# A hybrid decoder layer on one core: when the second attention's keys and queries are scaled

## The chip, the cores and the metric

The kernel runs on one core of one Trainium2 chip. The metric is the device time of one execution in microseconds (us); the number for a kernel is the median of its runs. A profile is one execution with every instruction's start and duration. Engines are named as in the profile: PE is the matrix engine and PEld its weight load, DVE the vector engine, ACT the scalar engine, POOL the GpSimd engine, SP the engine that issues most of the DMAs.

## What is computed

One layer on x of 512 tokens by 1024 features, in float32. The input is normed and multiplied by one wide matrix, whose columns feed four branches: a forgetting attention (8 heads of 64), a gated linear recurrence, a sparse attention (8 query heads on 2 key heads, over compressed blocks, selected blocks and a window), and a spatial gating unit. Each branch is gated, projected and added up, and one output projection is added to x. The change touches the sparse attention only:

```python
def rms_norm(x, g):
    x32 = x.astype(jnp.float32)
    y = x32 * lax.rsqrt(jnp.mean(x32 * x32, axis=-1, keepdims=True) + NORM_EPS)
    return (y * g.astype(jnp.float32)).astype(x.dtype)
...
y_c = nsa_attention(rms_norm(heads(qc, NSA_HEADS), qn_c), ..., kn_c, ...)
    # inside: rms_norm(k_slc, kn_g) and rms_norm(k_win, kn_g)
```

So 8 query heads and 4 key heads (2 selected, 2 window) of each token are divided by their root mean square.

## The kernel before

**Products.** Every float32 matrix product is made of three passes over pairs of rounded parts (high by high, low by high, high by low). A unit of dense work is three matmuls of 128x128 weights on 512 columns; the code counts it as `G` = 0.68. A dense product of the input matrix (`zgen` or `chunks`) loads a weight half by DMA into a raw buffer, rounds it to the high part on POOL or ACT (`hi_cast`), makes the low part by a subtraction on DVE (`wsplit`), and runs its units; the last unit of a bank is followed by its eviction.

**Two attentions with dense work between.** The first attention (`fox_units`, tiles `s_a`, `p_a`, `o_a`) and the second (`nsa_units`, tiles `s_s`, `p_s`, `s_w`, `p_w`, `o_s`) are chains of small steps on all engines. A call `fill(us)` puts so many microseconds of dense units from a queue between two steps (`step` takes one). Small jobs (generators in the list `side`) advance by one `yield` with each dense unit. In the queue during the first attention stand, in order, the keys and values `kv` (bank `z_kv`), the queries `qc` (bank `z_qc`), `cm0` (`z_cm`), `vd` (`z_vd`), then `ga`, and behind the first attention more `ga`, `gd` and `ud`.

**The order.** Within both attentions the instructions are not issued as they are written. `Order.add` collects them with what each needs; `Order.plan` walks a model of the engines in time and on each engine takes, among the instructions that can start, the one written first; `Order.settle` issues the result. The engines run their queues in this order, so an instruction that comes later than the model thought holds up everything behind it on its engine. The first settle is at the end of the first attention (`shut(r1)`), the second at the end of the second.

**What the change touches.** `emit_kv` and `emit_z` copy keys (`zkm`, rows named `zk_c` in the code) and queries (`zq_c`) out of their banks on ACT, square them on ACT (`sq`) and sum each head's squares on DVE into `ssc`. `nsa_scales` then makes 48 inverse roots per token row: a scaling of `ssc` and eleven small dependent DVE instructions of `rsqrt` on the tile `tsc`, and then eight POOL multiplications that scale keys and queries in place, four of 256 and four of 512 elements per partition. In the kernel before it is called behind the first attention:

```python
    kts = [k_tiles(rp2, nm) for nm in "sw"]
    nsa_scales()
    ...
    side.append(compress())
    later(*silu("ga", y["a"], range(2, 4)), *(zgen(f"gd{i // 2}", i % 2, gd_use(i)) for i in range(4)),
          *(zgen(f"ud{i // 2}", i % 2, ud_use(i)) for i in range(4)))
    fill(5 * G)
    k_operand(zk_c, 0, KNC, kts[0], "s")
    fill(2 * G)
    q0 = q_operand(zq_c, 0, QNC, "c0")
    fill(6 * G)
```

`k_operand` and `q_operand` turn the scaled keys and queries on PE (`kt_s`, `qt_c`) and make the attention's operands of them on ACT, DVE and POOL (`ka_s`, `kb_s`, `q_c`). `compress` is a side job that makes the compressed keys and values (`w_w1k`, `hpsk` and others).

Of the kernel before, what the change touches and what calls it, by code (L numbers as in the profile page):

```python
# [66 lines left out]
class Order:  # L67
# [30 lines left out]
    def add(self, name, method, args, kw):  # L98
        aps = [(n == 0, a) for n, a in enumerate(args)] + [(k in ("out", "accum_out"), a) for k, a in kw.items()]
        aps = [(w, a) for w, a in aps if isinstance(a, bass.AP)]  # L100
        n, need = len(self.ops), {}
        boxes = [(w, *self.area(a)) for w, a in aps]
        for w, t, *box in boxes:
            if w and t in self.before:
                need.update((m, True) for m, *_ in self.seen.get(self.before[t], ()))
            for m, w2, b in self.seen.get(t, ()):
                if (w or w2) and box[0] < b[1] and b[0] < box[1] and box[2] < b[3] and b[2] < box[3]:
                    need[m] = need.get(m, False) or not (name == "PE" == self.ops[m][0] and w and w2)
        if self.queued is not None and self.ops[self.queued][0] == name:
            need.setdefault(self.queued, False)  # L110
        for w, t, *box in boxes:
            self.seen.setdefault(t, []).append((n, w, box))
        self.ops.append((name, method, args, kw, need, self.cost(name, method, kw, aps), {b[1] for b in boxes},
                         {b[1] for b in boxes} & self.psum))
        self.pending.append(n)
        return n
# [23 lines left out]
    def plan(self):  # L140

        ops, left, then, ready = self.ops, {}, {}, {}
        soon, able = {e: [] for e in self.eng}, {e: [] for e in self.eng}
        free, end, out = dict(self.free), self.end, []
        wire, shared, load, bank = self.wire, self.shared, self.load, dict(self.bank)
        margin = lambda e, m: self.WAKE[e] + (self.MARGIN[e] if ops[m][0] not in (e, "SP") else 0.0)
        for i in self.pending:
            name, need = ops[i][0], ops[i][4]
            ready[i], left[i] = 0.0, 0
            for m, whole in need.items():  # L150
                if m in end:
                    ready[i] = max(ready[i], end[m] + margin(name, m) if whole else 0.0)
                else:
                    left[i] += 1
                    then.setdefault(m, []).append(i)
            if not left[i]:
                heapq.heappush(soon[name], (ready[i], i))
        done, todo = {}, len(self.pending)
        while len(out) < todo:
            best = None  # L160
            for e in self.eng:
                t = free[e]
                while soon[e] and soon[e][0][0] <= t:
                    heapq.heappush(able[e], heapq.heappop(soon[e])[1])
                c = (t, e) if able[e] else (soon[e][0][0], e) if soon[e] else None
                best = min(best, c) if best and c else best or c
            t, e = best
            while soon[e] and soon[e][0][0] <= t:
                heapq.heappush(able[e], heapq.heappop(soon[e])[1])
            i = heapq.heappop(able[e])  # L170
            open_ = max((bank[x][1] + self.WAKE[e] for x in ops[i][7] if x in bank and bank[x][0] != e), default=0.0)
            if open_ > t:
                heapq.heappush(soon[e], (open_, i))
                continue
            a, b = ops[i][5]
            if e == "PE":
                start = max(t + b, load)
                load, free[e], done[i] = start + a + 0.014, start + max(a - 0.098, 0.003), start + a + 0.172
            elif e == "SP":
                wire = max(wire, t + 1.3) + b  # L180
                free[e], done[i] = t + a, wire + 0.86
            else:
                done[i] = t + a
                if b:
                    if shared[1] != e and shared[0] > t + 0.06:
                        done[i] = shared[0] - 0.06 + a
                    shared = done[i], e
                free[e] = done[i] - self.OVER[e]
            for x in ops[i][7]:
                bank[x] = e, done[i]  # L190
            out.append((i, dict(free), wire, shared, load, done[i]))
            for j in then.get(i, ()):
                f = ops[j][0]
                ready[j] = max(ready[j], done[i] + margin(f, i) if ops[j][4][i] else t)
                left[j] -= 1
                if not left[j]:
                    heapq.heappush(soon[f], (ready[j], j))
        return out
# [48 lines left out]
def tile_hybrid_layer(ctx: ExitStack, tc: tile.TileContext, x, xT, units, small, bsp, out):  # L247
    nc = tc.nc
    order = Order(nc)
# [5 lines left out]


    def behind(op):
        return order.behind(op) if order.on else tc.issue_after(op)

    def shut(stack):  # L260

# [125 lines left out]
    def chunks(key, lhs_h, lhs_l, emit, fetch=None):  # L387

        banks = []

        def chunk(c):
            hi, lo = (fetch or wsplit)(f"{key}.{c // 2}", c % 2)
            yield AHEAD
            if c == 0:
                banks[:] = four(f"z_{key}")
            by_k = fetch is not None and c == 0
            for t, k2 in [(t, j) for j in range(2) for t in range(4)] if by_k else [(t, j) for t in range(4) for j in range(2)]:
                ts_ = slice(t * P, (t + 1) * P)
                k = 2 * c + k2
                cs = slice(k2 * S, (k2 + 1) * S)  # L400
                PE.matmul(banks[t], lhsT=lhs_h[:, k, ts_], rhs=hi[:, cs], start=k == 0, stop=False)
                PE.matmul(banks[t], lhsT=lhs_l[:, k, ts_], rhs=hi[:, cs], start=False, stop=False)
                PE.matmul(banks[t], lhsT=lhs_h[:, k, ts_], rhs=lo[:, cs], start=False, stop=k == KD - 1)
                if k == KD - 1:
                    emit(t, banks[t])
                yield G

        return [chunk(c) for c in range(4)]
# [19 lines left out]
    queue, owed, side = [], [0.0], []  # L428

    def later(*gens):  # L430
        queue.extend(Dense(g) for g in gens)
# [35 lines left out]
    def rsqrt(v, y, t):  # L467

        I32 = mybir.dt.int32
        DVE.tensor_scalar(t.bitcast(I32), v.bitcast(I32), 1, None, op0=ALU.logical_shift_right)  # L470
        DVE.tensor_scalar(y.bitcast(I32), t.bitcast(I32), -1.0, float(0x5F3759DF), op0=ALU.mult, op1=ALU.add)
        for _ in range(3):
            DVE.tensor_tensor(t, y, y, op=ALU.mult)
            DVE.scalar_tensor_tensor(t, t, -0.5, v, op0=ALU.mult, op1=ALU.mult)
            DVE.scalar_tensor_tensor(y, t, 1.5, y, op0=ALU.add, op1=ALU.mult)
# [92 lines left out]
    def emit_z(z, ss, c0, n, sqpool):  # L568
        def emit(t, ps):
            ACT.copy(z[:, t, 0:64 * n], ps[:, 0:64 * n])  # L570
            sq = sqpool.tile([P, S], F32, tag="ft", bufs=3, name=f"sq{c0}{t}")
            ACT.activation(sq[:, 0:64 * n], ps[:, 0:64 * n], AF.Square)
            DVE.tensor_reduce(ss[:, t, c0:c0 + n], sq[:, 0:64 * n].rearrange("p (h d) -> p h d", d=64),
                              axis=AX.X, op=ALU.add)
        return emit
# [109 lines left out]
    ap = pool("ap", att)  # L685
# [137 lines left out]
    def nsa_scales():  # L823
        DVE.tensor_scalar(ssc, ssc, 1.0 / 64, EPS, op0=ALU.mult, op1=ALU.add)
        y_ = tsc[:, 0, :].rearrange("p (t h) -> p t h", t=4)
        rsqrt(ssc, y_, tsc[:, 1, :].rearrange("p (t h) -> p t h", t=4))
        for t in range(4):
            for z, c0, n in ((zk_c, 0, 4), (zq_c, 4, 8)):
                zv = z[:, t, :].rearrange("p (h d) -> p h d", h=n)
                POOL.tensor_tensor(zv, zv, y_[:, t, c0:c0 + n].unsqueeze(2).to_broadcast([P, n, 64]), op=ALU.mult)  # L830

    zcm = [zkm[:, 2 + b, :] for b in range(2)]

# [18 lines left out]
    ACT.copy(kts[0][1][64:104, 0, :], f32(nb))  # L852
    for e, o in ((0, 64), (1, 0)):
        POOL.tensor_scalar(kts[1][1][o:o + 40, e, :], f32(nb), 1.0, 0.0, op0=ALU.mult, op1=ALU.add)
    later(*chunks("kv", xh, xl, emit_kv), *chunks("qc", xh, xl, emit_z(zq_c, ssc, 4, 8, ap)),
          zgen("cm0", 0, cm_use(0)), zgen("cm0", 1, cm_use(1)))
    vds = chunks("vd", xh, xl, emit_vd)
    later(*vds)
# [255 lines left out]
        return lambda ps: ACT.copy(ug["t"][:, i, :], ps)  # L1114

    kts = [k_tiles(rp2, nm) for nm in "sw"]
    nsa_scales()
    sgd = {}

    def gd_use(i):  # L1120
# [642 lines left out]
```

## Time and profile before

| | |
|---|---|
| median of 3 runs | 712.65 us (712.14 to 713.6) |
| profiled execution, its own time | 713.0 us |
| its span, first to last instruction | 711.3 us |
| PE busy | 700.0 us (98%), 3357 matmuls |
| DVE busy | 571.0 us (80%) |
| ACT busy | 362.3 us (51%) |
| POOL busy | 171.2 us (24%) |
| granted PE clock | 1.000 |

Between the span and the execution's own time lie 1.7 us that the engines' instructions don't cover. In the profile's rows the first two numbers are the start and the duration in us; a row of the windows gives, for a stretch of time, each engine's busy time and its instructions in brackets. Behind a row of the timeline stands in square brackets how long the engine was idle before it and who ended that. On the time axis the first attention lies at 80 to 202 us, the passage to the second at 200 to 240, and the second ends at 383.

### The profile page before, as it was taken

The page shows a single profiled execution, that of the slowest core. Times are in us where ns is not written, and L with a number is a line of the kernel's source. Part 1 is how long each engine was busy: PE and PEld are TensorE (multiplying, and loading weights), DVE is VectorE, ACT ScalarE, POOL GpSimd, SP SyncE. Part 2 cuts the span into 40 slices and gives each one's busy share as a digit, 9 for nine tenths or more (in the row PEclk, how much of TensorE's full clock was granted, in tenths as well). Part 3 has the DMA queues.
Part 4 walks back from the last instruction along what each step waited for, and adds up shares of the span by engine and source line. Part 5 has one row for each costly group of instructions (what it writes and reads, how often), then busy time and mean ns, then how long its engine had stood idle before and what let it go on. Part 6 is the DMA issues. An engine that isn't in the chain of part 4 may idle for free.

```text
span 711.3 us, 9561 instructions
## 1 busy us (share of the span) xinstructions
PE 700.0 (98%) x3357; PEld 573.4 (81%) x3357; DVE 571.0 (80%) x1090; ACT 362.3 (51%) x677; POOL 171.2 (24%) x230
## 2 busy tenths in 40 slices
PE   8999999999999999999999999999999999999997
PEld 6888778887877888888777888888888888888876
DVE  5799676677389949889897879999778858958995
ACT  4552555675524237776566881434534551653641
POOL 4124652453346303333244312100000000000000
PEclk9999999999999999999999999999999999999999
DMA  8613132111113431100201232333522333133302
GB/s 312 240 59 119 39 110 90 60 60 62 58 60 127 141 118 60 59 31 4 87 29 60 83 110 80 102 126 138 178 93 85 113 125 112 36 119 119 118 30 88
DMA packets 20640, 68.35 MB, mean 96 GB/s; under 512 B 2416, under 2 KB 2800, under 8 KB 20592
## 3 DMA queue, kind: packets, MB, share of 16 engines
q1 hardware_dynamic: 20160, 67.25, 28.4%
q8 instruction: 26, 0.43, 0.2%
q10 hardware_dynamic: 432, 0.49, 0.2%
q14 instruction: 22, 0.18, 0.1%
HBM read 65.64 MB, written 2.10 MB: 95 GB/s over the span
## 4 chain that ended last, share of the span: by engine, by line
PE 78%; DVE 13%; issue 3%; ACT 3%; DMA 2%; POOL 2%; SPq 0%; DVEq 0%; POOLq 0%; ACTq 0%
PE pj L223 9%; PE z_mg L223 6%; PE tb L211 3%; PE z_qc L211 3%; PE z_ud L211 3%; PE z_gb L223 3%; PE z_qa L211 3%; PE z_va L211 3%; PE o_s L211 3%; PE mg2y L223 2%; PE z_vd L211 2%; PE mg1y L223 2%; PE z_xb L211 2%; PE z_ka L211 2%; PE z_kv L211 2%
## 5 line engine op out<-in xcount | busy, mean ns | idle before, releaser
L223 PE MATMUL pj<-w_wb,yh 128*128 128x512 f32 x256 | 79.8, 389 | 0.0
L223 PEld LDWEIGHTS pj<-w_wb,yh 128*128 128x128 f32 x256 | 48.1, 188 | 9.9
L223 PE MATMUL pj<-w_wb,yl 128*128 128x512 f32 x128 | 49.8, 389 | 0.0
L223 DVE TENSOR_TENSOR w_wb<-r_wb,w_wb 128x512 fp32r<-128x512 f32 x32 | 20.9, 686 | 9.5 <-ACT w_wb L223 8.5
L223 PEld LDWEIGHTS pj<-w_wb,yl 128*128 128x128 f32 x128 | 24.0, 188 | 4.9
L211 POOL TENSOR_SCALAR p_w<-p_w,nm_w 128x128 f32<-128x128 f32 (+3 forms) x32 | 16.8, 543 | 39.2 <-DVE nm_w L211 39.2
L211 DVE TENSOR_TENSOR pl_a<-tb,ph_a 128x512 fp32r<-128x512 f32 (+1 forms) x24 | 14.4, 598 | 14.2 <-ACT ph_a L211 14.0
L211 ACT CAST ph_a<-tb 128x512 fp32r<-128x512 f32 (+1 forms) x24 | 12.4, 517 | 23.3 <-PE tb L211 23.1
L211 PE MATMUL z_xb<-xh,w_xb 128*128 128x512 f32 x64 | 24.0, 409 | 0.0
L211 ACT ACTIVATE p_s<-p_s,nm_s 128x512 f32<-128x512 f32 (+3 forms) x32 | 17.8, 559 | 11.8 <-DVE nm_s L211 11.1
L211 PE MATMUL z_gd<-xh,w_gd 128*128 128x512 f32 x64 | 22.7, 403 | 0.9 <-DVE w_gd L211 0.8
L211 ACT ACTIVATE p_w<-p_w,nm_w 128x512 f32<-128x512 f32 (+3 forms) x32 | 17.9, 561 | 10.2 <-DVE nm_w L211 10.1
L211 POOL TENSOR_SCALAR p_a<-p_a,nm_a 128x128 f32<-128x128 f32 (+3 forms) x32 | 19.7, 633 | 12.7 <-DVE nm_a L211 12.0
L211 PE MATMUL z_ud<-xh,w_ud 128*128 128x512 f32 x64 | 22.6, 400 | 0.0
L211 POOL TENSOR_SCALAR p_s<-p_s,nm_s 128x128 f32<-128x128 f32 (+3 forms) x32 | 17.3, 560 | 21.3 <-ACT ph_w L211 8.0
L211 ACT ACTIVATE p_a<-p_a,nm_a 128x512 f32<-128x512 f32 (+3 forms) x32 | 17.9, 560 | 7.0 <-DVE nm_a L211 6.9
L211 PE MATMUL z_ga<-xh,w_ga 128*128 128x512 f32 x64 | 21.3, 398 | 0.0
L211 DVE CUSTOM_DVE_ANT_0 p_a<-s_a,maskm 128x512 f32<-128x512 f32 (+3 forms) x32 | 15.3, 486 | 7.4 <-PE s_a L211 4.0
L223 PE MATMUL z_gb<-xh,w_gb 128*128 128x512 f32 x64 | 21.1, 390 | 0.0
L223 ACT CAST w_wb<-r_wb 128x1024 fp32r<-128x1024 f32 x12 | 12.6, 1047 | 15.5 <-issue 15.5
L211 DVE CUSTOM_DVE_ANT_0 p_s<-s_s,maskm 128x512 f32<-128x512 f32 (+3 forms) x32 | 15.0, 485 | 4.3 <-PE s_s L211 3.8
L211 DVE TENSOR_TENSOR pl_w<-tb,ph_w 128x512 fp32r<-128x512 f32 (+1 forms) x24 | 14.0, 598 | 3.0 <-ACT ph_w L211 2.8
(812 smaller groups left out, 2323.8 us busy)
## 6 DMA issues: line engine op xcount, KB each, us to landing
r_wb<-in_units_dram SPq DMA_DIRECT2D x16, 512.0 KB, 3.7
xt<-in_x_dram SPq DMA_DIRECT2D x4, 512.0 KB, 8.4
r_ga<-in_units_dram SPq DMA_DIRECT2D x4, 512.0 KB, 3.7
r_gd<-in_units_dram SPq DMA_DIRECT2D x4, 512.0 KB, 3.9
r_ud<-in_units_dram SPq DMA_DIRECT2D x4, 512.0 KB, 4.2
r_gc<-in_units_dram SPq DMA_DIRECT2D x4, 512.0 KB, 3.7
r_xb<-in_units_dram SPq DMA_DIRECT2D x4, 512.0 KB, 3.8
r_gb<-in_units_dram SPq DMA_DIRECT2D x4, 512.0 KB, 3.8
```

The costliest lines, as they stand in the source:

```text
L211: getattr(self.eng[name], method)(*args, **kw)
L223: return lambda *args, **kw: real(*args, **kw).ins
```

## The change

`nsa_scales` becomes a generator. The eviction of the last query bank (`last_qc`, row block t = 3) puts it into `side`, so that its DVE part is collected right behind that eviction and its eight POOL multiplications follow at one for every two dense units, amid the first attention. The call behind the first attention goes. Two further edits are in the planner's helper: what an instruction needs because its tile takes over an older tile's buffer is now looked up when the plan is made, and not when the instruction is collected; and `behind` accepts an instruction's number outside the planned part.

```diff
@@ Order.add
         for w, t, *box in boxes:
-            if w and t in self.before:
-                need.update((m, True) for m, *_ in self.seen.get(self.before[t], ()))
@@ Order.plan
             name, need = ops[i][0], ops[i][4]
+            for t in ops[i][6]:
+                need.update((m, True) for m, *_ in self.seen.get(self.before.get(t), ()))
@@ behind
-        return order.behind(op) if order.on else tc.issue_after(op)
+        if order.on:
+            return order.behind(op)
+        return nullcontext() if isinstance(op, int) else tc.issue_after(op)
@@ nsa_scales
         rsqrt(ssc, y_, tsc[:, 1, :].rearrange("p (t h) -> p t h", t=4))
+        yield 0.0
         for t in range(4):
             for z, c0, n in ((zk_c, 0, 4), (zq_c, 4, 8)):
                 zv = z[:, t, :].rearrange("p (h d) -> p h d", h=n)
                 POOL.tensor_tensor(zv, zv, y_[:, t, c0:c0 + n].unsqueeze(2).to_broadcast([P, n, 64]), op=ALU.mult)
+                yield 0.0
+                yield 0.0
@@
-    later(*chunks("kv", xh, xl, emit_kv), *chunks("qc", xh, xl, emit_z(zq_c, ssc, 4, 8, ap)),
+    emit_qc = emit_z(zq_c, ssc, 4, 8, ap)
+
+    def last_qc(t, ps):
+        emit_qc(t, ps)
+        if t == 3:
+            side.append(nsa_scales())
+
+    later(*chunks("kv", xh, xl, emit_kv), *chunks("qc", xh, xl, last_qc),
           zgen("cm0", 0, cm_use(0)), zgen("cm0", 1, cm_use(1)))
@@
     kts = [k_tiles(rp2, nm) for nm in "sw"]
-    nsa_scales()
     sgd = {}
```

## The prediction, made before the changed kernel ran

> **What bounds the kernel now.** I read the page first, then the windows of busy time, the groups of the tile `tsc`, and last the timelines of single engines.
>
> ```profile
> PE 700.0 (98%) x3357; PEld 573.4 (81%) x3357; DVE 571.0 (80%) x1090; ACT 362.3 (51%) x677; POOL 171.2 (24%) x230
> ```
>
> PE is busy for 700.0 of 711.3 us, and the change takes no PE work away. So the end moves only by the gaps between matmuls, those it closes and those it opens. The windows (PE, PEld, DVE, ACT, POOL busy, then clock, DMA share, GB/s) show where they lie:
>
> ```profile
> 140.00:170.00 30.00, 29.41 (x154) 24.47 (x153) 21.37 (x44) 17.78 (x40) 13.34 (x17) 1.00 0.22 71
> 200.00:210.00 10.00, 9.92 (x46) 7.75 (x45) 8.48 (x26) 2.75 (x5) 1.90 (x4) 1.00 0.19 63
> 210.00:220.00 10.00, 9.91 (x49) 7.82 (x48) 10.00 (x11) 2.17 (x4) 10.00 (x8) 1.00 0.44 148
> 220.00:230.00 10.00, 8.48 (x43) 6.14 (x42) 9.41 (x18) 4.85 (x13) 5.07 (x7) 1.00 0.28 89
> 230.00:240.00 10.00, 9.82 (x50) 8.04 (x49) 9.46 (x28) 4.20 (x7) 4.69 (x8) 1.00 0.57 178
> 240.00:400.00 160.00, 158.88 (x867) 131.26 (x866) 132.93 (x356) 99.87 (x250) 52.79 (x79) 1.00 0.18 60
> ```
>
> The passage between the attentions (200 to 240) has 0.08 + 0.09 + 1.52 + 0.18 = 1.87 us without PE. From 210 to 220 POOL and DVE are both busy all the time, and right behind it PE stands still. The groups of `tsc` say what POOL does there:
>
> ```profile
> L211 POOL TENSOR_TENSOR zkm<-zkm,tsc x4: 1056/1362/2058, 209.5 to 217.5; 128x256 f32<-128x256 f32 x4
> L211 POOL TENSOR_TENSOR zq_c<-zq_c,tsc x4: 1039/1263/1490, 211.5 to 218.6; 128x512 f32<-128x512 f32 x4
> L211 DVE TENSOR_TENSOR tsc<-tsc x3: 198/202/208, 203.3 to 207.2; 128x48 f32<-128x48 f32 x3
> ```
>
> These are the scales: eight POOL instructions from 209.5, over 10 us, behind a DVE chain of small instructions of 0.2 us. Now the timelines of PE and DVE behind it:
>
> ```profile
> 222.27 0.40 PE L211 MATMUL z_gd<-xh,w_gd 128*128 128x512 f32 x1
> 222.50 0.40 PE L211 MATMUL z_gd<-xl,w_gd 128*128 128x512 f32 x1
> 223.56 0.47 PE L211 MATMUL s_s<-ka_s,q_c 128*128 128x512 f32 x1 [0.67 <-DVE q_c L211]
> 223.87 0.40 PE L211 MATMUL s_s<-kb_s,q_c 128*128 128x512 f32 x1
> 224.35 0.41 PE L211 MATMUL s_s<-ka_s,q_c 128*128 128x384 f32 x1
> 224.60 0.34 PE L211 MATMUL s_s<-kb_s,q_c 128*128 128x384 f32 x1
> 225.71 0.73 PE L211 MATMUL z_gd<-xh,w_gd 128*128 128x512 f32 x2 [0.77 <-DVE w_gd L211]
> ...
> 218.12 2.55 DVE L211 TENSOR_TENSOR w_gd<-r_gd,w_gd 128x512 fp32r<-128x512 f32 x2
> 221.13 1.51 DVE L211 SCALAR_TENSOR_TENSOR kb_s<-kt_s,cc,ka_s 64x512 fp32r<-64x512 f32 x2 [0.45 <-ACT ka_s L211]
> 222.67 1.53 DVE L211 SCALAR_TENSOR_TENSOR q_c<-qt_c,cc,q_c 64x512 fp32r<-64x512 f32 x2
> 224.24 1.42 DVE L211 TENSOR_TENSOR w_gd<-r_gd,w_gd 128x512 fp32r<-128x512 f32 x1
> ```
>
> Matmuls of 512 columns follow each other at 0.23 us (222.27, 222.50) though each lasts 0.40, so a wait costs more than the gap shown. By starts, with 0.17 for 384 columns (an estimate, 0.23 x 384 / 512), lost are 223.56 - 222.73 = 0.83, 224.35 - 224.10 = 0.25 and 225.71 - 224.77 = 0.94. DVE's queue is late: `kb_s` waits for ACT's `ka_s`, that for the last turned keys, and the half `w_gd` that dense work needs stands behind `q_c`. Two more matmuls in the passage are late by starts, this one by 0.25 (211.61 against 210.90 + 0.46):
>
> ```profile
> 210.90 0.61 PE L211 MATMUL z_ga<-xh,w_ga 128*128 128x512 f32 x2
> 211.61 0.33 PE L211 MATMUL kt_s<-identf,zkm 128*128 128x128 f32 x1
> ```
>
> and this one by about 0.34 (0.18 and the 0.16 by which a matmul outlasts its turn):
>
> ```profile
> 233.71 0.50 PE L211 MATMUL z_gd<-xh,w_gd 128*128 128x512 f32 x1 [0.18 <-DVE sgd L211]
> ```
>
> Together the passage loses 2.6 us to these five.
>
> **The change part by part.** *Twelve DVE instructions leave the passage:* one on `ssc`, eleven on `tsc`, each 0.2 us long by the rows above; with overlap at start and end they hold DVE for less, so 12 x 0.2 = 2.4 us at most, and I take half, 1.2 (an estimate). What POOL does to DVE beside them:
>
> ```profile
> 210.40 0.68 DVE L211 TENSOR_TENSOR w_gd<-r_gd,w_gd 128x512 fp32r<-128x512 f32 x1
> ...
> 211.60 1.50 DVE L211 TENSOR_TENSOR w_gd<-r_gd,w_gd 128x512 fp32r<-128x512 f32 x1
> ```
> ```profile
> 211.51 1.04 POOL L211 TENSOR_TENSOR zq_c<-zq_c,tsc 128x512 f32<-128x512 f32 x1
> ```
>
> *Eight POOL instructions leave it too.* The same subtraction takes 0.68 us at 210.40 and 1.50 us at 211.60, where it ends 0.55 behind POOL's end at 212.55: it was held up for 0.8 us. The pair at 218.12 lost 2.55 - 2 x 0.68 = 1.2 more. With others between them I put the relief of DVE at 2 to 4 us, beside the 1.2. DVE has 40 us there and is busy 37.35; relieved of 4 or more it has slack. Keys and queries are then ready before the passage begins, `kt_s` waits for nothing, and `ka_s`, `kb_s`, `q_c` come early. What is late next is `sgd` (0.34), which I leave in half. Gain: 0.25 + 0.83 + 0.25 + 0.94 = 2.27 at most, or 2.6 with `sgd`; some of the lateness is `w_gd`'s own, so I take **2.2 us**; ends 0.5 (only the two waits on the keys' path that are shortest, 0.25 each) and 2.6.
>
> *They arrive in the first attention,* behind the last reduction on the queries (DVE, POOL, PE, then a group of `z_vd`):
>
> ```profile
> 143.87 0.67 DVE L211 TENSOR_REDUCE ssc<-sq 128x8 f32<-128x512 f32 x1
> ...
> 158.21 2.12 DVE L211 TENSOR_TENSOR w_vd.10_881<-r_vd.10_880,w_vd.10_881 128x512 fp32r<-128x512 f32 x2 [0.37 <-ACT w_vd.10_881 L211]
> ...
> 162.95 0.69 DVE L211 TENSOR_TENSOR pl_a<-tb,ph_a 128x512 fp32r<-128x512 f32 x1
> ```
> ```profile
> 158.85 1.96 POOL L211 TENSOR_SCALAR q_a<-q_a 64x512 fp32r<-64x512 f32 x2
> ```
> ```profile
> 162.71 0.40 PE L211 MATMUL o_a<-ph_a,v_a 128*128 128x512 f32 x1
> 163.70 0.66 PE L211 MATMUL tb<-identf,p_a 128*128 128x128 f32 x4 [0.59 <-DVE pl_a L211]
> ...
> 166.68 0.39 PE L211 MATMUL s_a<-ka_a,q_a 128*128 128x512 f32 x1
> ```
> ```profile
> L211 PE MATMUL z_vd<-w_vd.10_881,xh x16: 387/397/476, 172.6 to 180.7; 128*128 128x512 f32 x16
> ```
>
> From 140 to 170 POOL is busy 13.34 of 30 us, so eight at about 1.05 (their shortest times above), 8.4 us, fit. Queued on POOL behind a scale may stand a rounding of weights, the queries' copies (`q_a`, done at 160.81, wanted at 166.68: 5.9 us to spare) or the scaling of `p_a`. The weights have more: `w_vd.10` is ready at 160.33 and first used at 172.6. A POOL queue late by 2 or 3 us therefore costs nothing, and the cover is gone beyond 6. DVE is the thin place: the transposes `tb` of one piece of `p_a` wait for the `pl_a` of the piece before with no dense work put between, and once already, at 163.70, PE lost 163.70 - 162.94 = 0.76 us, when `w_vd.10` held DVE 2.12 us instead of 1.36. I take **one more stall of this kind, 0.76 us**; ends: minus 0.76 (the shifted order removes the one that is there) and four of them, 3.0.
>
> *No DMA moves;* the scales issue none, and SP's queue keeps its order. Raw buffers are freed earlier in the passage as DVE catches up, which costs nothing. *The two planner edits* add needs that the first writer of a new tile already waited for, so nothing by themselves. *The order after the passage* is planned afresh from other times: the 1.1 us without PE between 240 and 400 may become 0.4 or 1.8; I take zero, plus or minus 0.7.
>
> Sum: -2.2 + 0.76 = **-1.44 us**. Against the profiled execution's own 713.0 (711.3 span and 1.7 around it) that is 711.56; this execution lies 0.35 above the median, 712.65, so the median goes to **711.2 us**.
>
> **A rule against it.** A DVE instruction that reads two SBUF tensors was slowed beside POOL's scaling (1.50 against 0.68). The Trainium skill, "SBUF — State Buffer", section "Who interferes with whom", says such an instruction and a GpSimd one that reads SBUF exclude each other for the whole instruction; the trace's end 0.55 us behind POOL's agrees. By that rule the change moves the exclusion and removes none, and the sum would be near zero; by the rows above, where the weights lie ready 12 us ahead, the same holding costs less there. It speaks for the first rival.
>
> **Rivals.** *Moved, not removed.* DVE is held up in the first attention as it was in the passage, 2 to 4 us, and `pl_a` is late two or three more times: 2.2 gained, 3 x 0.76 = 2.3 lost, **712.7 us**. For it speaks 163.70; against it DVE's busy 21.37 of 30 us there, against 37.35 of 40 in the passage.
>
> *Slower: `pl_a` behind POOL.* Each of the eight POOL instructions holds a subtraction that stands in front of a `pl_a`. Eight stalls cost 6.1 us, less 2.2: at worst 716.5; five, taken as the middle of this case, 3.8 - 2.2 = +1.6: **714.3 us**. It decides from three stalls on, where the gain is used up. Against it: DVE instructions on PSUM (`pl_a`) are not slowed (0.69 at 162.95), and `vd` has four weight halves only in that stretch.
>
> *More.* The passage loses nothing and the second attention's order falls well: -2.6 - 0.7 = -3.3: **709.3 us**.
>
> **How the numbers follow.** About 0.2% (1.43 us) is what a measurement of this kernel can tell from no change. Forecast 0.48 (own range 709.9 to 712.2; 0.34 beyond the bound, 0.14 within); more 0.11, faster; moved 0.24 (0.22 within, 0.02 slower); slower 0.17 (0.16 and 0.01). That makes faster 0.45, same 0.37, slower 0.18. The range holds "more" but for its far end and leaves out the worse half of "slower": 709.0 to 714.2.
>
> **What would show it.** Right: `zkm<-zkm,tsc` on POOL at 145 to 165; PE without gaps at `s_s` and `z_gd` in the passage; `kt_s` about 7 us earlier; DVE's `w_gd` at 0.68. Wrong: gaps at `tb` behind `pl_a` from 145 to 175, `q_a` or `w_vd` late on POOL, or the same gaps in the passage with DVE still full, which would mean its lateness wasn't the scales'.

## The result and the profile after

The changed kernel takes 708.61 us (median; 708.35 to 708.8), the kernel before on the same chip 712.74 us; the ratio is 0.9941, 95% interval 0.9924 to 0.9958. It is faster by 4.1 us. The forecast was 711.2 with a range from 709.0 to 714.2: the sign was right, the size not, and the result lies 0.4 us below the range. The profiled execution has its own time of 708.75 and a span of 707.0 us.

The page's engines line and the windows of busy time of the changed kernel:

```profile
PE 697.3 (99%) x3357; PEld 574.0 (81%) x3357; DVE 567.8 (80%) x1090; ACT 361.6 (51%) x677; POOL 171.0 (24%) x230
```
```profile
140.00:170.00 30.00, 30.00 (x158) 25.32 (x158) 24.04 (x56) 17.96 (x41) 21.79 (x25) 1.00 0.20 64
200.00:210.00 10.00, 9.92 (x49) 8.27 (x49) 8.97 (x17) 5.34 (x8) 4.21 (x6) 1.00 0.32 107
210.00:220.00 10.00, 10.00 (x52) 8.53 (x51) 9.34 (x21) 4.71 (x12) 0.80 (x3) 1.00 0.32 104
220.00:230.00 10.00, 10.00 (x50) 8.38 (x49) 8.86 (x12) 1.59 (x3) 7.57 (x9) 1.00 0.46 145
230.00:240.00 10.00, 10.00 (x51) 8.22 (x50) 9.30 (x36) 2.80 (x8) 1.50 (x1) 1.00 0.56 188
240.00:400.00 160.00, 158.82 (x865) 131.22 (x864) 132.30 (x345) 101.94 (x253) 53.49 (x79) 1.00 0.19 59
```

The same instructions are there, in the same number. PE has lost its gaps in two places: in the first attention (140 to 170, 30.00 where it was 29.41) and in the passage (from 210 to 240 there is no gap left, and 200 to 210 keeps its 0.08). Behind 240 PE is busy as before (158.82 us of 160, where it was 158.88). DVE, though, is hardly less busy in the passage: 36.47 us of 40 where it was 37.35 (36.89 in a second profile of the changed kernel).

Two milestones of PE say how much each place gave. First the kernel before, then the changed one, by the groups of the tiles `o_a` and `z_ud` (the last figure before the semicolon is the start of the last one):

```profile
L211 PE MATMUL o_a<-pl_a,v_a x32: 274/402/481, 106.6 to 201.1; 128*128 128x512 f32 x8, 128*128 128x384 f32 x8, 128*128 128x128 f32 x8, 128*128 128x256 f32 x8
L211 PE MATMUL z_ud<-xl,w_ud x32: 387/393/400, 246.0 to 272.2; 128*128 128x512 f32 x32
```
```profile
L211 PE MATMUL o_a<-pl_a,v_a x32: 274/402/481, 106.6 to 200.2; 128*128 128x512 f32 x8, 128*128 128x384 f32 x8, 128*128 128x128 f32 x8, 128*128 128x256 f32 x8
L211 PE MATMUL z_ud<-xl,w_ud x32: 387/393/401, 241.1 to 267.9; 128*128 128x512 f32 x32
```

The first attention ends 0.9 us earlier, and the last product of the dense work behind it 4.3 us earlier: 0.9 from the first attention, 3.4 from the passage, and at the end of the kernel it is still 4.3 (711.3 to 707.0). The 0.9 is no chance of one profile: from the first of these `o_a` to the last it is 94.5 us in the kernel before, 93.6 in the changed one, and 93.5 or 93.6 in all versions below with the roots and the multiplications early at the planner's usual margin.

The scales are where the change puts them. Groups of `tsc` on POOL in the changed kernel, then PE in the passage:

```profile
L211 POOL TENSOR_TENSOR zkm<-zkm,tsc x4: 607/609/614, 151.7 to 157.6; 128x256 f32<-128x256 f32 x4
L211 POOL TENSOR_TENSOR zq_c<-zq_c,tsc x4: 1037/1268/1748, 152.2 to 163.2; 128x512 f32<-128x512 f32 x4
```
```profile
202.89 0.60 PE L211 MATMUL kt_s<-identf,zkm 128*128 128x128 f32 x4
...
211.05 0.39 PE L211 MATMUL z_ga<-xl,w_ga 128*128 128x512 f32 x1
211.28 0.39 PE L211 MATMUL s_s<-ka_s,q_c 128*128 128x512 f32 x1
211.50 0.39 PE L211 MATMUL s_s<-kb_s,q_c 128*128 128x512 f32 x1
```

The keys are turned at 202.89, 8.7 us earlier, and the first scores `s_s` come 12 us earlier, without a gap: 0.23 us behind the matmul before. The weights of the gating unit aren't held any more; DVE in the changed kernel has a pair at 1.29 us where before one stood at 2.55:

```profile
212.49 1.29 DVE L211 TENSOR_TENSOR w_gd<-r_gd,w_gd 128x512 fp32r<-128x512 f32 x2
```

In the first attention, `w_vd.10` holds DVE for 1.29 us where it was 2.12, but it also starts 0.6 later, and `pl_a` is only 0.2 us earlier than it was (162.76 against 162.95). Yet the stall at 163.70 is gone. DVE and PE in the changed kernel show why: three dense matmuls stand between `o_a` and `tb`, where there were none.

```profile
158.83 1.29 DVE L211 TENSOR_TENSOR w_vd.10_881<-r_vd.10_880,w_vd.10_881 128x512 fp32r<-128x512 f32 x2 [0.18 <-ACT w_vd.10_881 L211]
...
162.76 0.69 DVE L211 TENSOR_TENSOR pl_a<-tb,ph_a 128x512 fp32r<-128x512 f32 x1
```

```profile
162.75 0.39 PE L211 MATMUL o_a<-ph_a,v_a 128*128 128x512 f32 x1
162.97 0.39 PE L211 MATMUL z_vd<-w_vd.01_872,xh 128*128 128x512 f32 x1
163.20 0.39 PE L211 MATMUL z_vd<-w_vd.01_872,xl 128*128 128x512 f32 x1
163.43 0.39 PE L211 MATMUL z_vd<-w_vd.01_872,xh 128*128 128x512 f32 x1
163.66 0.60 PE L211 MATMUL tb<-identf,p_a 128*128 128x128 f32 x4
```

### The profile page after: what moved, and what is told of

It is laid out like the page before. It is cut to its first block, busy times and chain, and to the rows that moved or that the text cites. A ratio compares the mean times of both kernels' runs of the same rounds, so it can differ in the third digit from the quotient of the medians.

```text
span 707.0 us, 9559 instructions
## 1 busy us (share of the span) xinstructions
PE 697.3 (99%) x3357; PEld 574.0 (81%) x3357; DVE 567.8 (80%) x1090; ACT 361.6 (51%) x677; POOL 171.0 (24%) x230
## 4 chain that ended last, share of the span: by engine, by line
PE 85%; DVE 9%; ACT 2%; POOL 1%; issue 1%; DMA 1%; SPq 0%; DVEq 0%; POOLq 0%; ACTq 0%
PE pj L223 12%; PE z_mg L223 6%; PE tb L211 3%; PE z_vd L211 3%; PE z_ud L211 3%; PE z_qc L211 3%; PE z_gd L211 3%; PE z_gb L223 3%; PE z_ga L211 3%; PE z_qa L211 3%; PE z_va L211 3%; PE o_s L211 3%; PE mg2y L223 2%; PE mg3y L223 2%; PE mg1y L223 2%; PE z_xb L211 2%
```

## The experiments

Three questions: what it is in the late scales that costs the passage 3.4 us; why the first attention gained where a loss was forecast; and whether the planner edits do anything. The medians of the kernel before beside the three sets of runs were 712.87, 713.03 and 713.04 us.

### The passage: the operands' lateness, and POOL's hold on DVE

**Without the eight multiplications** (kernel before, its call at the old place; keys and queries stay unscaled):

```diff
-        for t in range(4):
-            for z, c0, n in ((zk_c, 0, 4), (zq_c, 4, 8)):
-                ...
-                POOL.tensor_tensor(zv, zv, y_[:, t, c0:c0 + n]..., op=ALU.mult)
```

> The kernel before, its roots made behind the first attention as they were, but without the eight POOL multiplications: keys and queries stay unscaled, so this leaves out part of the computation. The first attention is untouched (0 us there). If the passage's loss comes from the multiplications, by whatever way, the 3.4 us by which z_ud ended earlier in the passage are nearly all there: 709.4 us. If the chain of twelve small DVE instructions is what makes DVE late, most of the loss stays: 711.5 to 712.7.

Measured: 709.03 us, ratio 0.9948 (0.9936 to 0.9959), 3.8 us faster. The windows:

```profile
140.00:170.00 30.00, 29.39 (x153) 24.51 (x152) 21.04 (x44) 17.97 (x39) 13.35 (x17) 1.00 0.21 71
200.00:210.00 10.00, 9.92 (x49) 8.12 (x49) 8.79 (x26) 4.98 (x8) 3.67 (x5) 1.00 0.21 66
210.00:220.00 10.00, 10.00 (x51) 8.37 (x51) 9.87 (x20) 4.29 (x11) 1.76 (x2) 1.00 0.29 97
220.00:230.00 10.00, 10.00 (x49) 8.33 (x48) 9.89 (x15) 2.63 (x6) 6.67 (x8) 1.00 0.47 151
```

All of the passage's big gaps close though the twelve DVE instructions are still in it, and DVE is busy 9.87 and 9.89 of 10 us; from 230 to 240 PE still lacks 0.18. So neither the load of the DVE chain nor a full DVE made PE wait. What did is bound to the multiplications: the time that they take, and that keys and queries wait for them and, through them, for the chain. Here the keys are turned at 203.5 and wait for neither, so this run doesn't part the two. The first attention keeps its stall (29.39), as it must. Not all of the 3.8 lies in the passage: behind 240 PE is busy 159.12 of 160, because two waits that the last part below prices at 0.8 us are gone here too. That leaves about 3.0 for the passage.

**The multiplications made, but nobody waits for them** (same place; they write to a buffer that nobody reads there, so keys and queries go on unscaled):

```diff
-                POOL.tensor_tensor(zv, zv, y_[:, t, c0:c0 + n]..., op=ALU.mult)
+                xv = xbt[:, t, 0:64 * n].rearrange("p (h d) -> p h d", h=n)
+                POOL.tensor_tensor(xv, zv, y_[:, t, c0:c0 + n]..., op=ALU.mult)
```

> The kernel before, but the eight POOL multiplications write to the unused tile xb, so that POOL and the shared reads are loaded as before while keys and queries don't wait (they stay unscaled: the scaling is left out of the result). If the loss is that keys and queries come late (theory: late operands), it goes: 709.4 to 710. If it is that POOL's multiplications hold DVE's two-input subtractions (theory: holding), it stays: 712 to 712.7. In between, shares of both.

Measured: 710.53 us, 0.997 (0.9959 to 0.998). Timelines of POOL, DVE and PE in this kernel, and behind them the same pair on DVE in the kernel without the multiplications:

```profile
216.03 2.94 POOL L211 TENSOR_TENSOR xb<-zq_c,tsc 128x512 f32<-128x512 f32 x2
```
```profile
216.54 2.98 DVE L211 TENSOR_TENSOR w_gd<-r_gd,w_gd 128x512 fp32r<-128x512 f32 x2
```
```profile
216.14 0.39 PE L211 MATMUL z_ga<-xh,w_ga 128*128 128x512 f32 x1
218.12 0.74 PE L211 MATMUL z_gd<-xh,w_gd 128*128 128x512 f32 x2 [1.59 <-DVE w_gd L211]
```
```profile
215.30 1.29 DVE L211 TENSOR_TENSOR w_gd<-r_gd,w_gd 128x512 fp32r<-128x512 f32 x2
```

This parts the loss. With the operands no longer late, 712.87 - 710.53 = 2.3 us come back, of which some 0.8 again lie behind 240 (159.14 of 160), so about 1.5 in the passage. What is left, 710.53 - 709.03 = 1.5 us, is one wait of PE for a pair of subtractions that starts 1.2 us later and takes 2.98 us beside POOL's multiplications and 1.29 without them: 1.7 us longer. The Trainium skill, "SBUF — State Buffer", section "Who interferes with whom", has a DVE instruction with two SBUF inputs contend with a GpSimd one that reads SBUF; this pair agrees, and the multiplications pay too (2.94 for two of 512 elements, against 2 x 1.04 at their shortest).

**Only the roots early** (old lookup; DVE's part behind the last query product, the multiplications behind the first attention):

```diff
+    def nsa_mults():      # the loop with the eight POOL.tensor_tensor
+        ...
+        if t == 3:
+            side.append(nsa_scales())
...
     kts = [k_tiles(rp2, nm) for nm in "sw"]
-    nsa_scales()
+    nsa_mults()
```

> The kernel before with only the twelve DVE instructions of the roots made early; the eight POOL multiplications stay behind the first attention, and the planner is as before. They can start about 8 us earlier in the passage, since they don't wait for the chain. Theory late operands: most of the passage's 3.4 us goes, and the first attention may win its 0.9 or not: 709 to 710.5. Theory holding: POOL still holds DVE's subtractions, at another time: 711.5 to 712.7.

Measured: 710.83 us, 0.9962 (0.9948 to 0.9975). It did not become the test that it was meant to be: with the roots there, the plan drew the multiplications forward, to 189 to 196 us, where nothing holds them (0.61 and 1.04 us). But they push POOL's roundings back, and those hold DVE as well. POOL, DVE and PE of this kernel:

```profile
207.29 1.37 POOL L211 TENSOR_SCALAR tblv<-trs 128x1024 fp32r<-128x1024 f32 x1
208.62 1.49 POOL L211 TENSOR_SCALAR w_w1k<-r_w1k 128x1024 fp32r<-128x1024 f32 x1
```
```profile
196.20 3.02 DVE L211 TENSOR_TENSOR y_a<-y_a,th_ga 128x512 f32<-128x512 f32 x1
199.15 0.68 DVE L211 TENSOR_TENSOR pl_a<-tb,ph_a 128x512 fp32r<-128x512 f32 x1
...
206.65 4.00 DVE L211 TENSOR_TENSOR w_ga<-r_ga,w_ga 128x512 fp32r<-128x512 f32 x3
```
```profile
199.88 0.44 PE L211 MATMUL tb<-identf,p_a 128*128 128x128 f32 x2 [0.78 <-DVE pl_a L211]
...
218.59 0.72 PE L211 MATMUL z_gd<-xh,w_gd 128*128 128x512 f32 x2 [1.30 <-DVE w_gd L211]
```

Three subtractions of 0.68 us take 4.00 beside POOL's roundings, everything behind them on DVE is 2 us late, and PE waits 1.30 at the same `z_gd`. What counts in the passage is how much POOL work of any kind runs beside DVE's two-input instructions ahead of `w_gd`. The same happens at the end of the first attention: beside POOL's roundings of `w_ga` and `tblk`, from 195.60 to 198.68, one multiplication on DVE takes 3.02 us (1.30 in the kernel before), `pl_a` stands behind it, and PE stalls 0.78 at `tb`. That is a stall of the kind which the prediction feared. It uses up what the gap at 163.70 gave: PE is busy 30.00 of 30 from 140 to 170, but from the first `o_a` to the last it is 94.6 us, as before.

### The first attention: load or order

**Both** (the changed kernel, with the old call kept as well, so the scales are made twice):

```diff
     kts = [k_tiles(rp2, nm) for nm in "sw"]
+    for _ in nsa_scales():
+        pass
```

> The changed kernel with the old call behind the first attention kept as well: roots and multiplications are made in both places (keys and queries are scaled twice, so the result is another). It shows the first attention with the added load by itself, beside a passage as before. If the 0.9 us won in the first attention come with the added work and its shifted order: 711.8 us and the last o_a at 200.2. If the added work costs there what the prediction said (one stall of 0.76 more): 713.5. If the old call alone decides the passage, the passage loses its 3.4 us again.

Measured: 712.81 us, 0.9993 (0.9983 to 1.0002), its runs scattered from 711.15 to 713.58. By the median nothing is won. The trace is of an execution of 711.57, one of the three shortest of eleven; why the others are longer isn't known. In this trace PE is busy 30.00 of 30 from 140 to 170 and 8.48 from 220 to 230, exactly as before. So in it the early scales cost nothing in the first attention, and the late ones cost what they cost.

**The planner's trust** (one number, in the kernel before: how much later than modelled PE takes another engine's result to be):

```diff
-    MARGIN = {..., "PE": 0.5}
+    MARGIN = {..., "PE": 1.0}
```

> The kernel before with one number of the planner changed: the margin that it adds to the end of another engine's instruction before PE may count on it, 1.0 us in place of 0.5. It tests why the stall of PE at `tb` (163.70 in before, 0.76 us) is gone in the changed kernel although `pl_a` is ready there at the same time. Theory, the order: the stall is there because the plan believes that `pl_a` is in time and so puts no dense matmul in front of `tb`; any plan that trusts it less closes the gap. Then PE is busy 30.0 us from 140 to 170 (29.4 before), some dense matmuls stand between `o_a<-ph_a` and `tb`, the passage from 200 to 240 loses what it lost, and the time is 712.1 us (711.2 to 712.9, about 0.8 below before's 712.9). Rival, the load: the stall goes only when the scales' instructions are on DVE and POOL in the first attention; then 140 to 170 keeps its gap and the time is 712.9 or, with the order worse elsewhere, up to 714.

Measured: 718.81 us, 1.0079 (1.0066 to 1.0091), slower by 5.8 and far from the 712.1 expected. Its windows, and what PE waited for behind 200 us (total, times, longest):

```profile
140.00:170.00 30.00, 30.00 (x160) 25.36 (x158) 20.49 (x46) 19.04 (x42) 13.42 (x17) 1.00 0.22 71
200.00:240.00 40.00, 37.03 (x174) 28.81 (x173) 36.45 (x75) 13.48 (x25) 23.30 (x25) 1.00 0.37 124
240.00:400.00 160.00, 153.48 (x845) 127.53 (x844) 130.30 (x349) 93.88 (x237) 54.86 (x79) 1.00 0.18 59
```
```profile
PE tb L211 <- POOL p_w L211: 2.3, 4, 1.0
PE g L223 <- DVE xcl L223: 2.2, 2, 1.8
PE kt_s L211 <- POOL zkm L211: 1.3, 1, 1.3
```

On the question it was run for, it is plain: with no scales in the first attention, the stall at `tb` is gone (30.00 of 30), and again three dense matmuls stand in front of `tb`. The stall is the plan's doing, not the load's. The time went elsewhere: a margin for all of PE also shifts what follows. From 240 to 400 PE lost 158.88 - 153.48 = 5.4 us, mostly to `p_w` in the second attention and to `xcl` behind it, and the passage lost 38.13 - 37.03 = 1.1 more than before, where it was expected to stay. Why these come late with this margin wasn't traced further.

**The same margin on the best version** (below):

> The scales collected behind the second bank of `cm0` with the old lookup of needs (707.45 us, the lowest so far) and the planner's margin at 1.0 us in place of 0.5. Theory, the order: with the scales early the gaps that a margin can close up to 240 us are closed already (30.00 of 30 from 140 to 170, 10.00 in each window of the passage), so it gains nothing there; what is left is some 3.3 us lost by the starts from 245 to 384, most of it at chains that dense work doesn't reach, so 707.4 us, 706.5 to 708.3. Rival: the stalls from 245 to 384 are of the kind at `tb`, and dense work put in front closes a third of them: 706.3 us.

Measured: 712.45 us, 0.9991 (0.9981 to 1.0). Neither theory held: the passage stays whole (40.00 of 40), but from 240 to 400 PE loses again (155.16 of 160). From 140 to 170 it loses 0.24 (29.76), at a `tb` behind `pl_a`: the higher margin doesn't close every gap of that kind.

### The planner edits, and the place of the call

**The old lookup with the early scales** (the changed kernel with the lookup of needs put back where it was):

```diff
@@ Order.add
+            if w and t in self.before:
+                need.update((m, True) for m, *_ in self.seen.get(self.before[t], ()))
@@ Order.plan
-            for t in ops[i][6]:
-                need.update((m, True) for m, *_ in self.seen.get(self.before.get(t), ()))
```

> The changed kernel with the planner's lookup of an older buffer's users put back to where it was; the scales stay early. If the lookup does nothing for the time, 708.6 us as the changed kernel; if it has part in the gain, up to 1 us more, 709 to 709.6.

Measured: 707.77 us, 0.9923 (0.991 to 0.9936). The changed kernel itself, run beside the following ones:

> The changed kernel once more, as the yardstick for the others of this call: 708.6 us, 4.1 below the kernel before.

Measured: 708.26 us, 0.993 (0.9918 to 0.9943). **The new lookup alone**, in the kernel before, where the scales stay late:

> The kernel before with the planner's lookup edit alone; the scales stay behind the first attention. With the scales early, taking this edit back was worth 0.8 us between two calls (708.61 and 707.77). If the lookup is what costs it, this kernel is slower than before by about the same: 713.5 us. If the edit only reshuffles the second attention, it can come out on either side within 0.7 us; as the prediction had it, 712.7.

Measured: 712.98 us, 0.9997 (0.9988 to 1.0006): nothing. **Another place, old lookup**: the scales collected behind the second bank of `cm0`.

```diff
             ACT.copy(zcm[b], ps)
+            if b == 1:
+                side.append(nsa_scales())
...
-        if t == 3:
-            side.append(nsa_scales())
```

> The changed kernel with the planner's lookup as before, and the scales collected behind the second bank of cm0, some 16 dense units later in the first attention. The passage's 3.4 us should be won in any case: the last o_a tells the first attention's share. If its 0.9 us are owed to one lucky order, they are lost here or turn into a loss: 708.7 to 709.5. If the earlier place has no part in it: 707.8.

Measured: 707.45 us, 0.9917 (0.9905 to 0.993), the lowest of all. **The same place, new lookup:**

> The scales collected behind the second bank of `cm0`, with the lookup of needs made when planning, as in the changed kernel. Beside the same with the old lookup (707.45 us) it repeats the test of that edit at another place of the scales. Theory: with the scales early the new lookup makes a worse order in the second attention wherever they are collected: 708.2 us, 707.9 to 708.7, the loss behind 240 us. Rival: the 0.5 to 0.8 us between the two lookups is the luck of one order; then it may come out anywhere from 707.0 to 707.8 here.

Measured: 708.58 us, 0.9934 (0.9921 to 0.9946). **All eight at once**, old lookup, behind the last query product:

```diff
                 POOL.tensor_tensor(zv, zv, y_[:, t, c0:c0 + n]..., op=ALU.mult)
-                yield 0.0
-                yield 0.0
```

> The scales collected all at once behind the last query bank: the changed kernel with the old lookup of needs and without the two steps between POOL's multiplications. It tests whether spreading them over dense work matters. Theory, late operands and POOL's holding in the passage: all that counts is that the eight multiplications are over before 200 us, and POOL has half its time free from 140 to 170, so the time is that of the scales early with the old lookup: 707.7 us, 707.0 to 708.5. Rival: eight in a row (6.6 us at 0.61 and 1.04) hold DVE's two-input subtractions in front of several `pl_a`, and PE loses 0.76 at each of two or three: 709.5 us, with PE under 29.0 of 30 us from 140 to 170.

Measured: 707.59 us, 0.9921 (0.9907 to 0.9934), with 30.00 of 30 from 140 to 170. Spreading the multiplications and choosing the exact place make no difference that these runs show: three versions with the old lookup take 707.45 to 707.77, three runs with the new one 708.26 to 708.61. The intervals of single pairs overlap, but the two groups don't, and the traces say where it lies. What PE waited for between 240 and 400, in the changed kernel and then in the one with the old lookup:

```profile
PE tb L211 <- POOL p_s L211: 0.5, 2, 0.3
PE tb L211 <- DVE pc L211: 0.3, 1, 0.3
PE s_w L211 <- DVE nm_w L211: 0.2, 1, 0.2
```
```profile
PE tb L211 <- POOL p_s L211: 0.5, 2, 0.3
```

Two waits, for `pc` and for `nm_w`, are in the kernel before, in the changed kernel and in all others with the new lookup. At the planner's usual margin they are gone with the old lookup wherever the keys are turned by 204 us: in the three versions here, without the multiplications, with these set aside, and with only the roots early. They are worth 0.3 + 0.2 and, by the prediction's measure, 0.16 more each: 0.8 us, and 708.26 to 708.61 against 707.45 to 707.77 is 0.5 to 1.2. So the change left some 0.8 us lying. Why the lookup, which should name needs that are met in any case, makes the plan keep these two waits stays open.

## Why the prediction was right and wrong

**The sign and the place of the gain: right.** The gaps at `s_s`, `z_gd` and `sgd` went, the keys were turned early, `w_gd` came at its own speed, and no DMA took anything back (none stands among PE's waits from 80 to 400 us). The cover named for POOL held: `w_vd.11` and `p_a` came later on POOL, and PE from 140 to 170 shows no gap.

**The first attention: the step that failed, by 1.7 us.** The prediction took one more stall of 0.76 us behind `pl_a`; measured is a gain of 0.9. It read 163.70 as DVE's lateness that more load would repeat. The row showed as much that the plan had put nothing between `o_a` and `tb`; the plan is made afresh with the scales in it, and it put dense matmuls there. The lower end, minus 0.76, "the shifted order removes the one that is there", was the right case, and it was written down as the end and not as the value. The higher margin closes the same gap without any scales. A stall of the feared kind does exist (0.78 us with only the roots early), but not in the changed kernel.

**The passage: the right mechanism, mis-sized by 1.2 us.** Forecast 2.2, at most 2.6; measured 3.4. The sum took five waits and left part of `sgd` and of `w_gd`'s lateness standing, where all five closed. The end of 2.6 was too low as well, and the kernel before shows most of what it missed:

```profile
204.04 0.39 PE L211 MATMUL z_ga<-xl,w_ga 128*128 128x512 f32 x1
204.42 0.73 PE L211 MATMUL z_ga<-xh,w_ga 128*128 128x512 f32 x2
204.99 0.40 PE L211 MATMUL z_ga<-xl,w_ga 128*128 128x512 f32 x1
...
233.71 0.50 PE L211 MATMUL z_gd<-xh,w_gd 128*128 128x512 f32 x1 [0.18 <-DVE sgd L211]
234.05 0.39 PE L211 MATMUL z_gd<-xl,w_gd 128*128 128x512 f32 x1
```

At 204.42 dense matmuls are late by 0.15 and then by 0.11, a wait that isn't among the five. And behind four of the five the next matmul is late too: 234.05 comes 0.34 behind 233.71, not 0.23, and the others lose 0.08, 0.08 and 0.11, together 0.4. With these, 2.6 becomes 3.2 to 3.3 (an estimate by starts).

**DVE's relief: not what happened.** Relief of 4 us or more and slack were forecast; DVE's busy time in the passage fell by 0.9 (0.5 in the second profile). It is as full as it was, with work that used to come later (the first `p_s` stands at 213.69 now and stood at 225.69). The kernel without multiplications says it again: DVE 9.87 of 10 us busy and PE without a gap. A full DVE was not the cost; being behind by some microseconds at `q_c` and `w_gd` was.

**"The two planner edits ... nothing by themselves": right in the kernel before (712.98), wrong beside the early scales**, where they stand for 0.8 us that wasn't gained. Against the kernel before this changes nothing, and so the term for the order after the passage, zero, came out at zero: 158.88 and 158.82 of 160.

**The rivals.** "Moved, not removed" and "Slower" both needed stalls behind `pl_a`, and there is none from 140 to 170. The prediction held against the exclusion that the weights lie ready early, but the trace gives another reason: the exclusion hardly came along. Beside the eight multiplications, from 151.67 to 158.76 and at 163.25, the only DVE instruction that is visibly longer is one subtraction of `w_vd.01`, 0.85 us for 0.68. DVE has few instructions there that read two SBUF tensors, and two of POOL's multiplications wait instead (1.49 and 1.75 us for 1.04). "More", 709.3, came nearest, and partly by luck: the passage did lose nothing from 210 us on, but the rest came from the first attention and not from the second.

## What to carry to other kernels

Where a step in front of a full engine is moved, ask who waits for its output and whom it holds while it runs, and price both; the engine's busy share says neither, as 9.87 of 10 us with no wait behind it shows. Where instructions are ordered by a planner, a stall of half a microsecond can be a choice of the plan and not a shortage, and a change of the plan may remove it, so it can't be multiplied by the added load before it is known which it is. Here the one at 163.70 was the plan's, and the one at 199.88 with only the roots early came from a held DVE. A planner's number that closes one gap must be judged over the whole kernel: one margin closed 0.8 us here and opened more than 6.

## What the runs showed of the hardware

POOL's multiplication of two tensors, with nothing beside it that reads two, takes 0.61 us for 256 and 1.04 us for 512 elements per partition; the kernel before had the first kind at no less than 1.06 and up to 2.06, so eight cost 6.6 us in the open and over 10 in the passage. It isn't only POOL's two-input form that holds DVE: beside its roundings, which read one tensor, three subtractions of 0.68 us took 4.00, and a multiplication of 0.68 took 3.02. The hold works both ways: in the kernel before, the subtraction at 210.40 kept its 0.68 us while the first multiplication beside it, from 209.49, took 2.06 for 0.61, and the one at 211.60 took 1.50 while POOL's kept its 1.04.
